# Two thirds of the recurrence's output projection taken out of the merge and done between the steps of the prompt's attention

## The chip, the cores and the metric

The kernel runs on one core of one Trainium2 chip. The metric is the device time of one execution in microseconds, the median of several. The engines are TensorE (PE, with its weight loads shown apart as PEld), VectorE (DVE), ScalarE (ACT), GpSimd (POOL) and SyncE (SP), which issues most of the transfers.

## What is computed

One step of a decoder layer with two branches over the same rows: latent attention (MLA) and a recurrence (RWKV-7). There are 1040 prompt rows (16 meta tokens and 1024 of the prompt) and 8 rows of a decoding batch. Both branches are projected to the model's 1024 columns, gated and added. Cut to what matters here:

```python
o_mla = attend(...).reshape(B, T, 8 * 64) @ lw['w_o_mla']          # 512 -> 1024
o_rwkv, wkv_new = rwkv_branch(rw_cols, shift0, wkv0, lw)           # a scan over the tokens
o_rwkv = o_rwkv.astype(x.dtype) @ lw['w_o_rwkv']                   # 512 -> 1024
g_mla, g_rwkv = jnp.split(jax.nn.sigmoid(gate_in), 2, axis=-1)
x = x + (g_mla * o_mla + g_rwkv * o_rwkv) @ lw['w_out']
x = x + jnp.square(jax.nn.relu(rms_norm(x, g_ffn) @ lw['w_up'])) @ lw['w_down']
```

The change concerns the product of the recurrence's rows with `w_o_rwkv`. The meta tokens' rows are dropped before the merge, so 1032 rows enter it; they lie along the free axis (the "columns" below), in three blocks `NBQ` of 344.

## The kernel before

Products keep float32's precision by splitting each operand into a rounded high part and a remainder: the cast to the high part is ScalarE's (`wh<-raw`, L119, or L1035), the remainder is a subtraction, mostly POOL's (L110), and `mm3` issues three products, high by high, low by high, high by low. All products that go through the helper have the line L102, so they are told apart by the tile they write.

The part of the program around the change has two stages. **The mixed stage.** `rwkv` (L808) walks through the segments of the recurrence (`for s in range(LAST + 1)`, segments 0 to 8; all but the last have two chunks of 64 tokens) and `chain_step` (L650) through the chunks. A chunk is a chain: the `zu` products read the state, VectorE and ScalarE copy and add, and the state of the next chunk comes out of the last `zu` group. `solve`, `solve2` and `prep` get later segments ready (`sv`, `sc` products) with VectorE's help. `post` (L690) normalizes a finished segment's rows and writes them to `orw` in DRAM; post(s-1) is called in segment s.

Beside it `fill` (L1982) advances the prompt's attention `mla` (L1365), one step for each step of `rwkv`. Attention goes head by head (8 heads) and block by block (3 blocks of up to 384 queries). `mla_head` loads and splits a head's K and Q, through one staging buffer (`mst`, tile `qkst`). `mla_max` (L1088) finds the row maxima of the *next* head: its `mx` products go into a PSUM pool of two banks, VectorE reduces them, and a transposed copy `mt` puts the maxima into Q's extra row. `mla_block` (L1133) computes the scores `at` in another pool of two banks, ScalarE takes the exponential to `P`, and the `pv` product sums over V in a single bank. When the recurrence is done, `fill` is emptied. A tile scheduler puts each engine's instructions in order when the kernel is built, by data dependencies, free buffers and the priorities set with `hi(...)`: the recurrence's (1500 to 3500) above the attention's. On the chip each engine then executes its own queue in that fixed order and waits at its head where something is not ready.

**The merge** (`stage_merge`, L1394). `rows(i, b, ...)` loads block i of the attention's rows `om` (b = 0, divided by the softmax sums through a broadcast load `rl`) or of the recurrence's rows `orw` (b = 1), and splits them into `x`. `chunk(m, i0, i1)` does output block m of 8 for the row blocks i0 to i1: it loads and splits two weights (`w_o`, the attention's and the recurrence's half), loads the gates `gt` and takes their tanh on ScalarE (L1443), makes 12 products of 344 columns per branch and row block, multiplies each result with its gate on VectorE, adds the two on POOL and splits the sum for the next product. The first three m run blocks 0 and 1 first (`MB` = 3, `MC` = 2), then block 2; the other five run all three blocks.

## Time and profile before

| | us |
|---|---|
| three runs | 2014.69, 2030.19, 2030.24 (median 2030.19) |
| the profiled execution, its own time | 2013.76 |
| its span in the trace | 2011.8 (41,500 instructions) |
| TensorE busy | 1854.2 |
| VectorE / POOL / ScalarE busy | 1319.1 / 953.3 / 737.0 |
| mean granted TensorE clock | 0.957 of full |

The span is the profiled execution from its first to its last instruction; times of instructions are counted from its start. TensorE's products are pipelined, so a busy share of 92% does not mean that it runs at its peak, and the busy times by tile of one stretch can add up to more than the engine's own. A granted clock of 1.00 is 2.4 GHz, 0.50 is 1.2 GHz.

### The profile page before, as it was taken

The page shows a single profiled execution, that of the slowest core. Times are in us where ns is not written, and L with a number is a line of the kernel's source. Part 1 is how long each engine was busy: PE and PEld are TensorE (multiplying, and loading weights), DVE is VectorE, ACT ScalarE, POOL GpSimd, SP SyncE. Part 2 cuts the span into 40 slices and gives each one's busy share as a digit, 9 for nine tenths or more (in the row PEclk, how much of TensorE's full clock was granted, in tenths as well). Part 3 has the DMA queues.
Part 4 walks back from the last instruction along what each step waited for, and adds up shares of the span by engine and source line. Part 5 has one row for each costly group of instructions (what it writes and reads, how often), then busy time and mean ns, then how long its engine had stood idle before and what let it go on. Part 6 is the DMA issues. An engine that isn't in the chain of part 4 may idle for free.

```text
span 2011.8 us, 41500 instructions
## 1 busy us (share of the span) xinstructions
PE 1854.2 (92%) x16508; PEld 1710.7 (85%) x16508; DVE 1319.1 (66%) x2212; ACT 737.0 (37%) x1516; POOL 953.3 (47%) x791
## 2 busy tenths in 40 slices
PE   8999889999989978989898899999999988999996
PEld 6989778889989866767666799999999988999995
DVE  6743556665446577877854554586666667869896
ACT  5442211122212234444445533533333333443354
POOL 4353534443313243334542543465565574645766
PEclk9998999999989978999899999999999998999998
DMA  4355555653433353332324733534443468454422
GB/s 167 115 189 179 181 208 185 216 195 135 142 102 113 92 141 79 82 92 47 84 62 121 233 116 128 167 106 149 143 147 131 147 185 301 138 170 133 130 85 85
DMA packets 209921, 282.64 MB, mean 140 GB/s; under 512 B 52960, under 2 KB 124536, under 8 KB 209600
## 3 DMA queue, kind: packets, MB, share of 16 engines
q1 hardware_dynamic: 198784, 237.66, 38.0%
q0 software_dynamic: 10944, 42.33, 6.3%
q8 instruction: 130, 2.13, 0.4%
q14 instruction: 63, 0.52, 0.1%
HBM read 197.61 MB, written 82.31 MB: 139 GB/s over the span
## 4 chain that ended last, share of the span: by engine, by line
PE 45%; DVE 13%; DMA 6%; issue 5%; POOL 4%; ACT 2%; SPq 1%; DVEq 0%; POOLq 0%; ACTq 0%
PE u L102 23%; PE mm L102 13%; DVE pr L576 2%; PE sv L102 2%; PE pv L102 2%; PE at L102 1%; PE zu L102 1%; DVE T L578 1%; POOL ul L110 1%; DVE x L1744 1%; PE sc L102 1%; PE mx L102 1%; DVE mpart L1117 1%; DVE c L1684 1%; ACT uh L1035 1%
## 5 line engine op out<-in xcount | busy, mean ns | idle before, releaser
L102 PE MATMUL mm<-h,wh 128*128 128x344 f32 (+1 forms) x1680 | 423.2, 334 | 17.2 <-ACT wh L119 8.3
L102 PEld LDWEIGHTS mm<-h,wh 128*128 128x128 f32 x1680 | 299.4, 194 | 29.2 <-ACT wh L119 8.4
L102 PE MATMUL mm<-h,wl 128*128 128x344 f32 (+1 forms) x840 | 275.7, 331 | 0.0
L110 POOL TENSOR_TENSOR wl<-raw,wh 128x512 fp32r<-128x512 f32 (+2 forms) x71 | 92.6, 1305 | 176.3 <-ACT wh L119 172.1
L102 PEld LDWEIGHTS mm<-h,wl 128*128 128x128 f32 x840 | 162.5, 194 | 2.5 <-issue 1.6
L119 ACT CAST wh<-raw 128x512 fp32r<-128x512 f32 (+2 forms) x118 | 70.6, 606 | 230.8 <-PE mm L102 165.0
L102 PE MATMUL u<-B11h,uh 128*128 128x258 f32 x448 | 130.3, 291 | 9.9 <-DVE c L1695 4.9
L102 PE MATMUL u<-T1h,uh 128*128 128x258 f32 x416 | 119.0, 286 | 11.7 <-ACT acc L1790 9.9
L102 PE MATMUL u<-B11h,ul 128*128 128x258 f32 x448 | 128.4, 286 | 0.0
L102 PE MATMUL u<-B11l,uh 128*128 128x258 f32 x448 | 128.1, 286 | 0.0
L102 PE MATMUL u<-T1l,uh 128*128 128x258 f32 x416 | 118.5, 285 | 0.0
L102 PE MATMUL u<-T1h,ul 128*128 128x258 f32 x416 | 118.3, 284 | 0.0
L1685 ACT ACTIVATE c<-c 128x516 f32<-128x516 f32 x64 | 40.7, 636 | 204.5 <-DVE c L1684 204.5
L102 PE MATMUL u<-B21h,uh 128*128 128x258 f32 x384 | 108.9, 284 | 1.5 <-ACT r L1670 1.0
L102 PE MATMUL u<-B21h,ul 128*128 128x258 f32 x384 | 108.7, 283 | 0.0
L102 PE MATMUL u<-B21l,uh 128*128 128x258 f32 x384 | 108.4, 282 | 0.0
L1267 DVE STREAM_TRANSPOSE T<-R 128x2560 f32<-128x2560 f32 (+1 forms) x32 | 80.9, 2558 | 34.6 <-DMA R<-cache,ix 32.6
L102 PE MATMUL mm<-x,wh 128*128 128x344 f32 x384 | 91.9, 325 | 9.4 <-ACT wh L119 5.5
L102 PEld LDWEIGHTS u<-B11h,uh 128*128 128x128 f32 x448 | 86.5, 193 | 12.7 <-ACT uh L1035 6.2
L102 PE MATMUL pv<-P,V 128*65 128x272 f32 (+5 forms) x288 | 93.0, 416 | 1.8 <-ACT P L1152 1.7
L1229 POOL DMA_INDIRECT R<-cache,ix x64 | 62.6, 978 | 63.0 <-PE dc L102 47.3
L102 PE MATMUL mm<-m,wh 128*128 128x344 f32 x384 | 90.3, 323 | 2.0 <-ACT wh L119 2.0
(511 smaller groups left out, 5761.8 us busy)
## 6 DMA issues: line engine op xcount, KB each, us to landing
raw<-w_in SPq DMA_DIRECT2D x70, 256.0 KB
A<-w_up SPq DMA_DIRECT2D x70, 256.0 KB
adT<-ts SPq DMA_DIRECT2D x64, 258.0 KB
br<-adT SPq DMA_DIRECT2D x64, 258.0 KB
a<-w_down SPq DMA_DIRECT2D x64, 256.0 KB
adB<-c SPq DMA_DIRECT2D x48, 258.0 KB
br<-adB SPq DMA_DIRECT2D x48, 258.0 KB
z<-zs SPq DMA_DIRECT2D x8, 1280.0 KB
```

Source lines behind the costliest of these rows:

```text
L102: self.nc.tensor.matmul(out, l, r, start=start, stop=stop)
L110: (eng or self.nc.vector).tensor_tensor(lo, src, hi.bitcast(F32), ALU.subtract)
L119: nc.scalar.copy(hi, raw)
L576: nc.vector.tensor_tensor(q, T[q_, :, 0:i + 1], Nt[q_, 0:i + 1, i].rearrange("p (o j) -> p o j", o=1).to_broadcast([q_.stop - q_.start, 8, ...
L578: nc.vector.tensor_reduce(T[q_, :, i], q, AX.X, ALU.add)
L1035: self.nc.scalar.copy(hi, src)
L1117: nc.vector.tensor_reduce(t[:m, j:j + 1], ps[:m, :n], AX.X, ALU.max)
L1229: self.nc.gpsimd.indirect_dma_start(out=R[:, 4 * i:4 * i + 4].rearrange("p a c -> p (a c)"), out_offset=None, in_=self.I["cache"].rearrang ...
L1267: nc.vector.transpose(t.rearrange("p j x k -> p x j k"), R[:, :, c0:c1].rearrange("p x (j c) -> p x j c", c=32))
L1684: V.scalar_tensor_tensor(c, c, 0.0, self.r2[:, ns], ALU.max, ALU.mult)
L1685: A.activation(c, c, AF.Square)
L1744: V.tensor_tensor(v2(t), ps, v2(t), op)
```

## The change

A new generator `rwkv_out` computes `w_o`'s recurrence half times the recurrence's rows for row blocks 0 and 1 (of three), output block by output block: it loads the rows from `orw` and splits them (`owh`, `owl`), loads and splits a weight for each of the 8 output blocks, makes 12 products of 344 columns into a tile `ow`, has ScalarE copy the result to `oo`, and writes that to a new DRAM buffer `ows`. `fill` advances it at every fourth step of the attention. A block may begin only when the rows it needs are written: `post` sets `ow_ready` to 1 behind segment 3's call and to 2 behind segment 6's.

In the merge, `chunk` no longer loads the recurrence's half of the weight unless the last row block is among its blocks, makes the recurrence's 12 products for row block 2 alone, and for blocks 0 and 1 loads the finished product from `ows` (`oa`) and multiplies it with the gate in one pass of 688 columns. That is 192 products of 576 fewer in the merge, and 192 more in the mixed stage.

The PSUM pools of the mixed stage change with it: instead of two banks for `at`, two for `mx` and one for `pv` there are four for `at`, `mx` and `ow` together and one for `pv`.

```diff
@@ -60,6 +60,8 @@
 RP = 300
 MC = 2
 G0, G1, F1, S0, MST = 8, 1000, 1, 5, 1
+
+OWS = (3, 6)
 RPS = (("sc", 1), ("sv", 1), ("zu", 1))
 
 V_GMIX, V_GQ, V_GKV, V_MU, V_W0, V_A0, V_KK, V_KA, V_RK, V_LNW, V_LNB, V_GFFN, V_GFIN = (
@@ -177,6 +179,7 @@
         self.om = d.tile([128, 4, TPAD], F32, name="om")
         self.qr = d.tile([2, 128, TPAD], F32, name="qr")
         self.dsm = d.tile([544, NS], F32, name="dsm")
+        self.ows = d.tile([KD, 128, 2 * 344], F32, name="ows")
         self.xs = d.tile([128, KD, TQ], F32, name="xs")
         self.ads = {n: d.tile([2 * KD, 128, HT], F32, name="ad" + n) for n in XO[0]}
 
@@ -838,6 +841,7 @@
         get = lambda s: prep[s] if s <= LAST else (None, none)
 
         def post(s):
+            self.ow_ready = (s > OWS[0]) + (s > OWS[1])
             if s >= 0:
                 with hi(1500):
                     self.post(prep[s][0])
@@ -1104,7 +1108,7 @@
             t = self.asm.tile([128, 3], F32, tag="mp", name="mpart") if len(bl) > 1 else None
             dst = mx[:m, i - i0, 0:1]
             for j, (k0, n) in enumerate(bl):
-                ps = self.ps_mx.tile([128, 512], F32, tag="mx", name="mx")
+                ps = self.ps_at.tile([128, 512], F32, tag="at", name="mx")
                 last = j == len(bl) - 1
                 self.mm(ps[:m, :n], Q[0:96, 128 * (i - i0):128 * (i - i0) + m], Kk[0][0:96, k0:k0 + n], True, not last)
                 if last:
@@ -1390,6 +1394,29 @@
                 pass
             V = nxt
 
+    def rwkv_out(self, ctx):
+
+        nc = self.nc
+        p = self.pool(ctx, "owp")
+        for i in range(2):
+            while self.ow_ready <= i:
+                yield
+            n0, n = NBQ[i]
+            hi, lo = (p.tile([128, 4, n], F32R, tag="x" + t, name="ow" + t) for t in "hl")
+            for k in range(4):
+                raw = self.rp.tile([128, 512], F32, tag="raw", name="raw")[:, :n]
+                nc.sync.dma_start(raw, self.orw[:, k, META + n0:META + n0 + n])
+                self.split(hi[:, k], lo[:, k], raw, nc.gpsimd)
+            for m in range(KD):
+                w = self.load_k(self.I["w_o"][m][:, 4:], 4, eng=nc.gpsimd)
+                ps = self.ps_at.tile([128, 512], F32, tag="at", name="ow")[:, :n]
+                for k in range(4):
+                    self.mm3(ps, w[k][0], w[k][1], hi[:, k], lo[:, k], k == 0, k == 3)
+                o = p.tile([128, 344], F32, tag="o", name="oo", bufs=2)
+                nc.scalar.copy(o, ps)
+                nc.sync.dma_start(self.ows[m, :, n0:n0 + n], o)
+                yield
+
 
     def stage_merge(self, ctx):
 
@@ -1429,22 +1456,27 @@
             for i in range(3):
                 with self.tc.high_priority(RP):
                     a = rows(i, 0, 0, 3)
-                    r = rows(i, 1, 0, 4)
+                    r = rows(i, 1, 0, 4) if i == 2 else None
                     z = rows(i, 0, 3, 4)
                 x.append(([a[j] + z[j] for j in range(2)], r))
 
             def chunk(m, i0, i1):
-                w = [self.load_k(I["w_o"][m][:, 4 * b:4 * b + 4], 4) for b in range(2)]
+                w = [self.load_k(I["w_o"][m][:, 4 * b:4 * b + 4], 4) for b in range(1 + (i1 == 3))]
                 a, z = NBQ[i0][0], sum(NBQ[i1 - 1])
                 gt = [gp.tile([128, TQ], F32, tag=f"gt{b}", name="gt")[:, :z - a] for b in range(2)]
                 for b in range(2):
 
                     nc.sync.dma_start(gt[b], self.gts[2 * m + b][:, a:z])
                     nc.scalar.activation(gt[b], gt[b], AF.Tanh, scale=0.5)
+                w_ = min(z, 688) - a
+                if w_ > 0:
+                    oa = gp.tile([128, 688], F32, tag="oa", name="oa")[:, :w_]
+                    nc.sync.dma_start(oa, self.ows[m, :, a:a + w_])
+                    nc.vector.scalar_tensor_tensor(gt[1][:, :w_], gt[1][:, :w_], 1.0, oa, ALU.add, ALU.mult)
                 for i in range(i0, i1):
                     n0, n = NBQ[i]
                     t = [gt[b][:, n0 - a:n0 - a + n] for b in range(2)]
-                    for b in range(2):
+                    for b in range(1 + (i == 2)):
                         self.proj(w[b], x[i][b], 4, lambda _, n0, n, ps: nc.vector.scalar_tensor_tensor(
                             t[b], t[b], 1.0, ps, ALU.add, ALU.mult), [(0, n)])
                     nc.gpsimd.tensor_tensor(t[0], t[0], t[1], ALU.add)
@@ -1982,14 +2014,19 @@
                 def fill():
                     yield from gates
                     ca.close()
-                    psum(cm, ("at", 2), ("mx", 2), ("pv", 1))
+                    psum(cm, ("at", 4), ("pv", 1))
                     with tc.high_priority(HP):
                         k.mla_open(cm)
                     smp = k.sample_step(c)
+                    ow = k.rwkv_out(cm)
                     for i, _ in enumerate(k.mla()):
                         if k.rwkv_done:
                             next(smp, None)
+                        if i % 4 == 3:
+                            next(ow, None)
                         yield
+                    for _ in ow:
+                        pass
                     for _ in smp:
                         yield
                 fill = fill()
```

**What moves in the queues.** The scheduler places the moved products, and with them everything else, anew. The first engine is TensorE. The counts give how many instructions of the attention (the masks' products included) and of `ow` stand in its queue ahead of the first `zu` product of a chunk:

| ahead of | before: at, mx, pv | after: at, mx, pv, ow |
|---|---|---|
| segment 4, first chunk | 96, 62, 25 | 75, 54, 21, 0 |
| segment 5, second chunk | 193, 96, 53 | 75, 54, 21, 0 |
| segment 7, second chunk | 344, 148, 96 | 185, 96, 53, 96 |
| segment 8, its only chunk | 489, 192, 138 | 185, 96, 53, 96 |
| the merge | 504, 192, 144 | 504, 192, 144, 192 |

In the rows below a name's number tells one tile from the next, `idb` is the identity, `mb` a mask, and `UV`, `BKt`, `AR`, `Sm`, `BK`, `TT` are the recurrence's operands; the helper's line L102 is L104 in the changed file.

The first place is in the recurrence's segment 5, on TensorE. Before, attention products stand between the chunk's `zu` and `sv`:

```order
L102 MATMUL at_10890<-Qh02_7627,Kh0_7623 128x272
L102 MATMUL at_10890<-Ql0_7631,Kh0_7623 128x272
L102 MATMUL at_10890<-Qh02_7627,Kl0_7633 128x272
L102 LDWEIGHTS idb_120
L102 MATMUL at_10890<-mb_7639,idb_120 128x128
L102 MATMUL zu_9128<-UV_8233,BKt_8232 64x64 x8
L102 MATMUL sv_9061<-AR_8844,BK_8851 128x128 x4
L102 MATMUL pv_10742<-P_10830,V_9458 65x272
L102 MATMUL at_10905<-Qh02_7627,Kh0_7623 128x256
L102 MATMUL at_10905<-Ql0_7631,Kh0_7623 128x256
L102 MATMUL at_10905<-Qh02_7627,Kl0_7633 128x256
```

After, the queue holds only the recurrence there, from segment 4's first chunk on (`zu_9625` opens the second chunk of segment 5), up to the first `ow` products, and the next `at` stands behind those:

```order
L104 MATMUL sv_9062<-AR_8845,BK_8852 128x128 x4
L104 MATMUL zu_9129<-UV_8234,BKt_8233 64x64 x8
L104 MATMUL sv_9068<-AR_8845,BK_8852 128x128 x4
L551 MATMUL sc_9332<-cst_120,BK_8852 128x128 x4
L104 MATMUL zu_9129<-Sm_8012,UV_8234 64x64 x8
L104 MATMUL sv_9074<-AR_8845,BK_8852 128x128 x4
L104 MATMUL zu_9625<-UV_8234,Sm_8012 64x64 x8
L104 MATMUL ow_9609<-owh_9585,wh_9604 128x344
L104 MATMUL ow_9609<-owl_9586,wh_9604 128x344
L104 MATMUL at_9682<-Qh11_7627,Kh1_7622 128x384
```

The attention's instructions of three chunks have moved behind the first `ow`.

The second place is where the attention goes from one head to the next, on TensorE, late in the stage. Before (seven more `at` tiles of this head stand ahead of these rows; `mx_11726` is the first product that needs the following head's K and Q):

```order
L102 MATMUL pv_11758<-P_11791,V_11467 65x384
L102 MATMUL at_11811<-Qh01_7626,Kh0_7623 128x256
L102 MATMUL at_11811<-Ql0_7631,Kh0_7623 128x256
L102 MATMUL at_11811<-Qh01_7626,Kl0_7633 128x256
L102 LDWEIGHTS idb_120
L102 MATMUL at_11811<-mb_7639,idb_120 128x128
L102 MATMUL mx_11726<-Kh1_7624,Qh10_7628 128x256
L102 LDWEIGHTS idb_120
L102 MATMUL mx_11726<-mb_7639,idb_120 128x256
L102 MATMUL mx_11738<-Kh1_7624,Qh10_7628 128x256
```

After, at a change of head in the stretch behind the recurrence (`mx_12115` is the first product with the next K and Q):

```order
L104 MATMUL pv_11988<-P_12049,V_11205 65x272
L104 MATMUL at_12107<-Qh00_7623,Kh0_7621 128x384
L104 MATMUL at_12107<-Ql0_7629,Kh0_7621 128x384
L104 MATMUL at_12107<-Qh00_7623,Kl0_7631 128x384
L104 LDWEIGHTS idb_121
L104 MATMUL at_12107<-mb_7637,idb_121 128x128
L104 MATMUL pv_11988<-P_12062,V_11205 65x272
L104 MATMUL pv_11988<-P_12077,V_11205 65x144
L104 MATMUL pv_11988<-P_12085,V_11205 65x16
L104 MATMUL pv_12106<-P_12112,V_11856 65x384
L104 MATMUL mx_12115<-Kh1_7622,Qh10_7626 128x256
```

Here one `at` tile of the new head stands ahead of the first `mx`, where eight did before, and the two kinds alternate from there.

The third place is the start of the merge, on ScalarE. Before (`ov` is the attention's last copy, `x1000` and `x1100` casts of the merge's rows, L710 to L715 the last segment's normalization):

```order
L1156 COPY ov_12096<-pv_12029 65x272
L1035 CAST x1000_12199<-raw_12189 128x1032
L1035 CAST x1100_12205<-raw_12203 128x1376
L710 ACTIVATE sq_10923<-y_10717 128x512
L1443 ACT_TABLE_LOAD
L1443 ACTIVATE gt_12269<-gt_12269 128x688
L1443 ACTIVATE gt_12270<-gt_12270 128x688
L1443 ACTIVATE gt_12349<-gt_12349 128x688
L1443 ACTIVATE gt_12350<-gt_12350 128x688
L714 ACT_TABLE_LOAD
L714 ACTIVATE sq_10923<-sv_10933,eps_62 128x512
```

After:

```order
L1160 COPY ov_12485<-pv_12418 65x272
L1470 ACT_TABLE_LOAD
L1470 ACTIVATE gt_12640<-gt_12640 128x688
L1470 ACTIVATE gt_12641<-gt_12641 128x688
L1470 ACTIVATE gt_12689<-gt_12689 128x688
L1470 ACTIVATE gt_12690<-gt_12690 128x688
L1039 CAST x0000_12554<-raw_12544 128x1032
L1039 CAST x0003_12568<-raw_12558 128x344
L1484 ACTIVATE m00_12520<-gt_12640 128x344
```

Two casts and the normalization with its table loads have left this place; a table load and four `gt` now stand ahead of the first cast `x0000`. SP's queue grows from 944 to 988 rows, 40 of its new transfers ahead of the merge: 8 loads of `orw`, 16 of `w_o` and 16 stores to `ows`.

## Rows read from the trace of the kernel before

**Rows 1.** Page, part 1: busy time of each engine, share of the span, instructions.

```profile
PE 1854.2 (92%) x16508; PEld 1710.7 (85%) x16508; DVE 1319.1 (66%) x2212; ACT 737.0 (37%) x1516; POOL 953.3 (47%) x791
```

**Rows 2.** By stretch: start:end length, busy PE PEld DVE ACT POOL, clock, DMA share, GB/s.

```profile
790.60:837.50 46.90, 45.28 (x598) 35.24 (x597) 38.38 (x102) 24.25 (x65) 19.32 (x18) 1.00 0.37 91
837.50:892.00 54.50, 47.36 (x591) 36.67 (x590) 39.37 (x103) 26.18 (x68) 21.31 (x20) 0.94 0.38 97
892.00:945.20 53.20, 48.17 (x584) 36.85 (x583) 43.00 (x118) 24.63 (x69) 20.29 (x19) 0.98 0.21 45
...
1015.00:1070.40 55.40, 51.46 (x506) 38.82 (x504) 33.77 (x89) 25.16 (x72) 19.84 (x22) 0.94 0.22 62
```

**Rows 3.** Timeline of TensorE, first groups of chunks: start, length, in brackets idle before.

```profile
837.52 0.73 PE L102 MATMUL zu<-UV,Sm 128*64 128x64 f32 x4
...
911.51 0.69 PE L102 MATMUL zu<-UV,Sm 128*64 128x64 f32 x16
...
1015.06 0.34 PE L102 MATMUL zu<-UV,Sm 128*64 128x64 f32 x4
...
1088.92 0.28 PE L102 MATMUL zu<-UV,Sm 128*64 128x64 f32 x2
...
1096.98 0.69 PE L102 MATMUL zu<-Sm,UV 128*64 128x64 f32 x16 [1.31 <-DVE PT L684]
1097.81 0.42 PE L102 MATMUL mm<-x,wh 128*128 128x344 f32 x1
```

**Rows 4.** TensorE alone in that stretch, by tile: at, mx, pv, zu, sv in order.

```profile
1015.00:1070.40 55.40, 27.06 (x118) 0.94 0.22 62
1015.00:1070.40 55.40, 12.21 (x46) 0.94 0.22 62
1015.00:1070.40 55.40, 21.10 (x66) 0.94 0.22 62
1015.00:1070.40 55.40, 3.86 (x80) 0.94 0.22 62
1015.00:1070.40 55.40, 6.68 (x192) 0.94 0.22 62
```

**Rows 5.** VectorE over 790.6 to 945.2, tile mx, then tile mt.

```profile
sum 154.60, DVE 34.69; mean DVE 11.56
sum 154.60, DVE 9.90; mean DVE 3.30
```

**Rows 6.** A stretch at low clock (columns as Rows 2), and a zu group in it.

```profile
738.00:779.00 41.00, 32.10 (x364) 25.42 (x364) 25.03 (x70) 10.57 (x28) 15.27 (x16) 0.62 0.29 71
...
741.08 1.12 PE L102 MATMUL zu<-Sm,UV 128*64 128x64 f32 x16
```

**Rows 7.** Timeline of ScalarE and POOL: a head's K and first block of Q.

```profile
1038.00 1.07 ACT L1035 CAST Kh<-qkst 96x1048 fp32r<-96x1048 f32 x1 [0.63 <-PE at L102]
1039.49 2.43 POOL L110 TENSOR_TENSOR Kl<-qkst,Kh 96x1048 fp32r<-96x1048 f32 x1
...
1046.29 0.51 ACT L1035 CAST Qh<-qkst 96x384 fp32r<-96x384 f32 x1 [0.42 <-DMA qkst<-qr]
```

**Rows 8.** The merge: mm products by stretch, longest wait, timeline, chain.

```profile
1097.80:1204.00 106.20, 94.77 (x576) 0.97 0.56 175
1150.00:1200.00 50.00, 50.00 (x319) 1.00 0.46 152
...
PE mm L102 <- ACT wh L119: 5.5, 1, 5.5
...
1103.85 1.28 ACT L1443 ACT_TABLE_LOAD   x1
...
1110.79 0.78 ACT L1443 ACTIVATE gt<-gt 128x688 f32<-128x688 f32 x1 [1.32 <-DMA gt<-gts]
...
1116.86 5.29 DMA rl<-rls
...
1122.30 2.07 POOL raw L1423
```

## The prediction

> **What bounds the kernel now.** Begin with the page's head: TensorE is busy for 92% of the span [rows 1], so work that only changes its place gains nothing unless it lands where TensorE waits. Next take the busy time of each engine by stretch. In the three segments of the recurrence between 790.6 and 945.2 us TensorE is busy for 45 to 48 us of 47 to 55 us, and VectorE, the second engine, for 38 to 43 us [rows 2]. Two independent streams fill that time: the recurrence, a dependent chain of small products (`zu`, `sv`, `sc`) with much VectorE work between them, and the prompt's attention (`at`, `mx`, `pv`), which fills the chain's gaps. The stage ends only when both are done, and in the trace they end together: the last chunk's last product starts at 1096.98, the merge's first at 1097.81 [rows 3]. The merge then keeps TensorE full (50.00 us of 50.00), 576 products in 106.2 us [rows 8]. So the merge is bound by TensorE, and the stage before it by TensorE as long as attention and recurrence run side by side. The order of each queue is fixed when the kernel is built, so what runs beside what is read from the order, and how long it takes from the trace.
>
> **The change, part by part.** I follow TensorE's queue from the first place where it departs.
>
> *The start of the hold.* The recurrence's chunk that opens segment 4 starts at 837.5 [rows 3]. Ahead of it the new order has 21 `at`, 8 `mx` and 4 `pv` fewer (the table of counts). At the prices derived under the tail these are 3.8 + 1.7 + 2.0 = 7.5 us of TensorE. Between no gain, where the chain sets the pace, and all of it, I take half: the chunk starts at 834 (830 to 838).
>
> *The hold.* From there to the second chunk of segment 5 the new order has no attention at all. The next `at` stands behind the first `ow` products, and these need the recurrence's rows of segments 0 to 3 to be written to DRAM, read back and split. So for three chunk steps TensorE has the recurrence alone. In the trace these steps took 911.5 - 837.5 = 74.0 us with the attention beside them [rows 3]. Alone they cannot be faster than VectorE: it was busy for 38.38 + 39.37 + 43.00 = 120.8 us over three segments [rows 2], at most 34.7 + 9.9 = 44.6 us of that for the attention's maxima [rows 5], which leaves 76.2 us, 25.4 us a segment and 38 us for one and a half. VectorE reached 120.8/154.6 = 78% in those stretches, because the chain makes it wait; 38/0.78 is 49, and I take 50 us. Bounds: 38 to 74.
>
> Here a page speaks against the change. The trace first: between 738 and 779 us, where TensorE was busy for only 32.1 of 41 us, the mean granted clock was 0.62, most of it the lower level, 1.2 GHz; a group of 16 `zu` products took 1.12 us there and 0.69 us at full clock [rows 3, 6]. The Trainium skill, TensorE: Matmul & The Clock Gate, in its part 1 on the clock gate, says that the throttled clock is the default and that activity releases it. The hold would then run at 1.2 GHz throughout. Five groups a chunk cost 5 x 0.43 = 2.2 us more, 6.5 us over three steps, and the forecast would rise by that. I leave it out, because the 78% already comes from a chain with such waits.
>
> *The shared stretch.* From the second chunk of segment 5 to the second of segment 7 both orders run both streams. Before: 1015.1 - 911.5 = 103.6 us [rows 3] with 151 `at`, 52 `mx`, 43 `pv`. Now 110, 42 and 32, and 96 `ow`. By the prices below that is 7.3 + 2.1 + 5.5 = 14.9 us of attention less and 15.1 us of `ow` more: 104 us. Bounds 89 (`ow` hidden in the chain's waits) to 119 (the lost attention gives nothing back).
>
> *The end of the recurrence.* At the second chunk of segment 7 the second hold begins, since the second half of `ow` needs the rows up to segment 6. Three chunks are left until the first `ow` of that half. The last chunk of the trace took from 1088.9 to the end of its last group, 1096.98 + 0.69 = 1097.7 us: 8.8 us [rows 3]; three of those are 26, with posts and the last solve between them I take 27 us. Bounds 23 to 45. The recurrence then ends at 834 + 50 + 104 + 27 = 1015 us, 82 us earlier than before, and at that point 319 of 504 `at`, 96 of 192 `mx`, 91 of 144 `pv` and 96 `ow` are still to do.
>
> *The tail.* The nearest rows are those of 1015 to 1070.4, where the attention was nearly alone. TensorE's busy time by tile is 27.06 + 12.21 + 21.10 + 3.86 + 6.68 = 70.9 us (products overlap) in 55.4 us [rows 4], so each of those us stands for 0.78 us. That is 0.179 us for one of 118 `at`, 0.207 for one of 46 `mx`, and 0.50 for a `pv`, which is two instructions in the trace (66 there). The tail: 57.1 + 19.9 + 45.5 = 122.5 us, and `ow` at the merge's own price of 50/319 = 0.157 us [rows 8] adds 15.1, in all 137.6 us. Two corrections. That stretch had a mean clock of 0.94 [rows 2]; full clock takes off about 3 us in 55, 7 in all. But `at` and `mx` now draw on one pool of four banks and stand alternately in the queue. At the change of a head only one `at` tile stands ahead of the next head's first `mx`, where before several stood there (the order's second place). That `mx` needs the next K and Q. In the trace, from the cast of K to the end of the first cast of Q took 1038.0 to 1046.8, 8.8 us, with the split of K and a load in between [rows 7]. One `at` tile and the four last `pv` cover about 3 us, so some 5 us stay open at each of three heads; at the fourth, `ow` products cover it. I take 14 us: 137.6 - 7 + 14 = 145 us. Bounds: 120 (full clock, no boundary waits) and 172 (four full waits). The stage ends at 1160 us, where it ended at 1097.8: **62 us later**.
>
> *The merge.* It loses 192 of its 576 products, 30.1 us [rows 8]. It also loses the wait of 5.5 us for a weight's cast [rows 8]: ScalarE had to do the last segment's rows and their table loads there, and these are now long done. Against this, ScalarE's new order has one table load and four `gt` behind the attention's last copy, 1.28 + 4 x 0.8 = 4.5 us [rows 8], then the first cast of `x`. Before, the first two blocks of `x` were cast ahead of that copy. The copies and splits of `raw` follow one another for three blocks, with 2.1 us for a POOL product and 5.3 us for a slow `rl` load as the trace's sizes [rows 8]. TensorE waits some 9 us. The merge also moves more bytes in less time: per output block, two weights of 256 KB, two `gt` of 528 KB and one `oa` of 352 KB in about 48 x 0.157 = 7.5 us is 256 GB/s, against 175 over the merge before [rows 8]; I take 3 us for late loads. The removed product passes on VectorE pay for the new pass over `oa`. Together: 106.2 - 30.1 - 5.5 + 9 + 3 is 82.6; less 3 us for the half-clock part that the merge had (mean clock 0.97 over 106.2 us [rows 8]), 79 us: **27 us shorter**. Bounds 22 to 34.
>
> *What costs nothing.* ScalarE (16 copies, 21 casts) and POOL (24 splits) do the rest in a stage where they are busy for less than 27 of 47 to 55 us [rows 2]. Their cover is that slack; gone, it would cost their 20 to 30 us. SP's queue gets 40 more transfers before the merge; the `raw` loads wait on it for the rows' landing, and segment 7's `Ns` stores queue behind them. That is inside the 78%.
>
> **Sum.** +62 - 27 = +35 us. The profiled execution took 2013.8 us by its own time, which gives 2049. The runs shown took 2014.7, 2030.2 and 2030.2; with the profiled one, two of four are 16 us above the others, which one profile cannot explain. I add half, 8 us: **2057 us**.
>
> **Rivals.**
> *No difference.* The recurrence alone may run at VectorE's floor (38 us), the shared stretch may hide `ow` (89 us), and the tail may run at 122 us. Then the stage ends at 834 + 38 + 89 + 27 + 122 = 1110, 12 us later, and the merge takes back 27: -15 us, about 2007 with the offset. For it speaks that the attention stretch was TensorE-bound at 51 of 55 us; against it that all three must come at their ends. With one or two of them the result lies between -15 and +20.
> *Faster.* One mechanism: the hold frees the chain entirely, and its three steps take the 8.8 us of the last chunk each, 26 us. With the shared stretch at 89 and the tail at 128, the stage ends at 834 + 26 + 89 + 27 + 128 = 1104 and the net is +6 - 27 = -21 us, 2001. It decides from a stage end before 1105. Against it: VectorE's 38 us do not fit in.
> *Slower still.* Every change of a head waits the full 8.8 us (tail 172) and the merge's loads, whose stage reached 0.56 of the DMA engines at 175 GB/s [rows 8], become its bound with no gain left beyond 22 us. +62 + 27 - 22 = +67, about 2089.
>
> **How the numbers follow.** My forecast, +20 to +55, gets 0.55, slower still 0.14, no difference 0.24, faster 0.07. About 1%, 20 us, is what a measurement of this kernel tells from no change. So slower 0.69, same 0.24, faster 0.07. The range leaves one in ten out at each side: from the middle of the no-difference case, 2014, to just above the slower one, 2096; these take in 16 us between like runs.
>
> **What would show it.** The hold: no `at` product for some 50 us from about 835 us, and the clock falling there. The recurrence's last `zu` near 1015 us, and 60% of the `at` products after it. The tail: some 145 us with TensorE waiting at heads 4 to 7 for the cast of Q. The merge's first product near 1170 and its length near 79 us. The forecast is wrong if the recurrence ends before 990 us, or if the tail takes under 125 us.

## The result, and the profile after

The changed kernel takes 2138.86 us (median of 4 runs, 2132.66 to 2139.32) against 2024.21 us before (4 runs, 2014.69 to 2030.24): the ratio is 1.058, 95% interval 1.054 to 1.062. The profiled execution took 2139.21 us with a span of 2137.1. It was forecast slower, at 2057, with a range to 2096: the direction was right, the size was not. The loss is 115 to 125 us, not 35.

One label of the table of counts has to be put right first, and with it the sentence that all segments but the last have two chunks: the segment with a single chunk is the first, and the row "segment 8, its only chunk" is segment 8's second chunk. The places and counts stand.

The page's first row, which answers [rows 1]:

```profile
PE 1904.3 (89%) x16508; PEld 1753.9 (82%) x16508; DVE 1320.4 (62%) x2201; ACT 753.0 (35%) x1549; POOL 972.8 (46%) x813
```

TensorE has the same 16508 instructions and is busy for 50 us more, since part of them now runs at a lower clock, and idle for 75 us more (232.8 against 157.6 us of the span). The stretches, with the columns of [rows 2]: the first hold, the shared stretch, the second hold, the merge, and the tail in a second answer:

```profile
837.60:909.00 71.40, 50.83 (x622) 43.87 (x623) 41.85 (x95) 20.68 (x49) 26.71 (x27) 0.55 0.35 88
909.00:1013.00 104.00, 92.18 (x1116) 75.48 (x1116) 78.02 (x191) 42.70 (x111) 52.05 (x52) 0.93 0.31 83
1013.00:1068.60 55.60, 34.26 (x490) 29.30 (x485) 20.82 (x48) 15.50 (x39) 19.80 (x25) 0.56 0.21 54
...
1220.20:1327.00 106.80, 71.91 (x386) 66.81 (x387) 53.07 (x78) 45.12 (x71) 47.98 (x38) 0.82 0.64 188
...
1068.00:1220.20 152.20, 132.12 (x746) 100.27 (x743) 50.11 (x128) 68.47 (x178) 36.40 (x29) 0.90 0.28 80
```

Both holds are where the order put them, and in both the clock is near its lower level: 0.55 and 0.56, where [rows 2] showed 0.94 to 1.00. But they are long. TensorE's timeline, which answers [rows 3], has their edges:

```profile
837.58 1.26 PE L104 MATMUL zu<-UV,Sm 128*64 128x64 f32 x12 [4.25 <-DVE Sm L649]
...
907.41 1.12 PE L104 MATMUL zu<-UV,Sm 128*64 128x64 f32 x16
908.46 0.66 PE L104 MATMUL ow<-owh,wh 128*128 128x344 f32 x1
...
1020.07 1.12 PE L104 MATMUL zu<-UV,Sm 128*64 128x64 f32 x16
...
1034.68 0.27 PE L805 MATMUL sc<-cst,yb 8*128 8x8 f32 x1 [4.86 <-DMA yb<-sy]
...
1068.14 0.65 PE L104 MATMUL ow<-owh,wh 128*128 128x344 f32 x1
...
1235.56 0.65 PE L104 MATMUL mm<-x,wh 128*128 128x344 f32 x1 [15.38 <-ACT x L1039]
```

The attention's last product ends at 1220.2, and TensorE then waits 15.4 us for the merge's first operand. The steps of the sum against the trace, each from the times above (and 1326.9, the end of the merge's last product; before, 1097.9 and 1204.3):

| step | forecast, us | measured, us | off by |
|---|---|---|---|
| start of the first hold | 834 | 837.6 | +4 |
| first hold | 50 | 907.4 - 837.6 = 69.8 | +20 |
| shared stretch | 104 | 1020.1 - 907.4 = 112.7 | +9 |
| end of the recurrence, to the next `ow` | 27 | 1068.1 - 1020.1 = 48.0 | +21 |
| tail | 145 | 1220.2 - 1068.1 = 152.1 | +7 |
| mixed stage against before | +62 | +122.3 | +60 |
| merge against before | -27 | 106.7 - 106.4 = +0.3 | +27 |
| the rest of the kernel | 0 | 810.2 - 807.5 = +2.7 | +3 |

So three terms carry the miss: the two holds, 41 us, and the merge, 27 us. The 4 us of the first row arose ahead of the stage, where the input projection ended at 726.4 instead of 722.3; counted from there the hold began 4 us sooner than before, as forecast.

### The profile page after: what moved, and what is told of

The parts are those of the page before. It is cut to its first block, busy times and chain, and to the rows that moved or that the text cites. A ratio compares the mean times of both kernels' runs of the same rounds, so it can differ in the third digit from the quotient of the medians.

```text
span 2137.1 us, 41651 instructions
## 1 busy us (share of the span) xinstructions
PE 1904.3 (89%) x16508; PEld 1753.9 (82%) x16508; DVE 1320.4 (62%) x2201; ACT 753.0 (35%) x1549; POOL 972.8 (46%) x813
## 5 line engine op out<-in xcount | busy, mean ns | idle before, releaser
L104 PE MATMUL mm<-h,wh 128*128 128x344 f32 (+1 forms) x1680 | 424.3, 334 | 18.8 <-ACT wh L121 7.7
L104 PEld LDWEIGHTS mm<-h,wh 128*128 128x128 f32 x1680 | 300.0, 195 | 31.2 <-ACT wh L121 7.8
L104 PE MATMUL mm<-h,wl 128*128 128x344 f32 (+1 forms) x840 | 275.8, 331 | 0.0
L112 POOL TENSOR_TENSOR wl<-raw,wh 128x512 fp32r<-128x512 f32 (+2 forms) x85 | 109.2, 1287 | 212.4 <-ACT wh L121 203.8
L104 PEld LDWEIGHTS mm<-h,wl 128*128 128x128 f32 x840 | 162.6, 194 | 2.5 <-issue 1.6
L121 ACT CAST wh<-raw 128x512 fp32r<-128x512 f32 (+2 forms) x131 | 78.9, 607 | 242.4 <-PE mm L104 162.6
L104 PE MATMUL u<-B11h,uh 128*128 128x258 f32 x448 | 129.2, 289 | 8.0 <-DVE c L1727 3.6
L104 PE MATMUL u<-T1h,uh 128*128 128x258 f32 x416 | 119.2, 287 | 13.0 <-ACT acc L1822 11.2
L104 PE MATMUL u<-B11h,ul 128*128 128x258 f32 x448 | 128.0, 286 | 0.0
L104 PE MATMUL u<-B11l,uh 128*128 128x258 f32 x448 | 127.7, 285 | 0.0
L104 PE MATMUL u<-T1l,uh 128*128 128x258 f32 x416 | 118.6, 285 | 0.0
L104 PE MATMUL u<-T1h,ul 128*128 128x258 f32 x416 | 118.5, 285 | 0.0
L104 PE MATMUL u<-B21h,uh 128*128 128x258 f32 x384 | 108.9, 284 | 1.6 <-ACT r L1702 1.2
L104 PE MATMUL u<-B21h,ul 128*128 128x258 f32 x384 | 108.8, 283 | 0.0
L104 PE MATMUL u<-B21l,uh 128*128 128x258 f32 x384 | 108.4, 282 | 0.0
L104 PE MATMUL mm<-x,wh 128*128 128x344 f32 x256 | 68.1, 350 | 34.0 <-ACT x L1039 27.1
L104 PEld LDWEIGHTS u<-B11h,uh 128*128 128x128 f32 x448 | 85.9, 192 | 10.1 <-ACT uh L1039 4.5
L104 PE MATMUL mm<-m,wh 128*128 128x344 f32 x384 | 91.0, 325 | 3.5 <-ACT wh L121 3.5
L104 PE MATMUL pv<-P,V 128*65 128x272 f32 (+5 forms) x288 | 90.6, 408 | 2.3 <-ACT ov L1160 2.2
```

The source lines that it names most:

```text
L104: self.nc.tensor.matmul(out, l, r, start=start, stop=stop)
L112: (eng or self.nc.vector).tensor_tensor(lo, src, hi.bitcast(F32), ALU.subtract)
L121: nc.scalar.copy(hi, raw)
```

## The experiments

In what follows "stage" is the time from the input projection's last product to the last product of recurrence, attention and `ow`, and "merge" the time from there to the merge's last product, both from the runs' profiled executions. Medians, with the kernel before run beside them (`oldpools` was run twice, the last four rows once each). The diffs show changed lines alone; what lies between them is left out.

| kernel | median, us | before beside it | ratio, 95% interval | stage, us | merge, us |
|---|---|---|---|---|---|
| before | | | | 375.6 | 106.4 |
| changed | 2138.86 | 2024.21 | 1.054 to 1.062 | 493.8 | 106.7 |
| oldmerge | 2144.21 | 2022.72 | 1.057 to 1.065 | 500.0 | 110.5 |
| newmerge | 2029.23 | 2022.72 | 1.000 to 1.005 | 384.6 | 104.0 |
| newmerge_pl | 2015.71 | 2019.73 | 0.995 to 1.000 | 388.4 | 83.9 |
| after_pl | 2130.10 | 2019.73 | 1.048 to 1.059 | 501.9 | 87.9 |
| oldpools | 2106.87 | 2020.93 | 1.039 to 1.046 | 461.5 | 108.2 |
| tail | 2081.75 | 2022.72 | 1.027 to 1.035 | 432.2 | 109.9 |
| tail22 | 2070.25 | 2022.72 | 1.019 to 1.028 | 423.9 | 112.0 |
| late22_pl | 2079.64 | 2020.93 | 1.027 to 1.032 | 446.8 | 87.8 |
| noatt | 1972.38 | 2020.93 | | 339.7 | 101.7 |
| noatt_fill | 1977.57 | 2018.61 | | 349.2 | 98.9 |
| nofill | 2145.88 | 2019.73 | | 504.6 | 107.2 |
| filler | 2148.73 | 2019.73 | | 502.7 | 105.8 |

**What sets the pace of the holds.** The kernel before, with the attention taken out:

```diff
-                    for i, _ in enumerate(k.mla()):
-                        if k.rwkv_done:
-                            next(smp, None)
-                        yield
+                    k.no_att(cm)          # om and ls filled with ones
+                    while not k.rwkv_done:
+                        yield
```

> The kernel before without the prompt's attention (its outputs are filled with constants): the recurrence has TensorE and VectorE to itself for its whole length. Theory V, the chain with its solves sets its own pace and the attention only filled its waits: the three chunks from segment 4's first to segment 5's second take 60 to 75 us, as with the attention beside them (74.0) and as in the changed kernel's hold (69.8), and the last chunks of segments 7 and 8 take some 45 us as in its second hold. Theory W, the step of the prediction, that the chain alone keeps VectorE at 78%: 50 us or less for the three chunks.

The same three chunks by the profile of `noatt`, and the rest up to the recurrence's end at 1062.7:

```profile
824.00:894.80 70.80, 50.70 (x606) 43.91 (x606) 38.56 (x88) 23.47 (x48) 21.68 (x21) 0.52 0.33 83
...
989.30:1062.70 73.40, 47.00 (x497) 41.82 (x497) 28.67 (x59) 27.16 (x46) 27.63 (x24) 0.60 0.38 93
```

Alone the three chunks take 70.8 us, beside the attention 74.0 [rows 3], in the hold 69.8. Theory V holds for them; W falls. Two of the kernels below, `tail` and `late22_pl`, have no hold at this place, and there the same chunks run beside the attention:

```profile
831.60:901.00 69.40, 64.48 (x784) 49.93 (x783) 54.05 (x140) 35.30 (x93) 32.75 (x30) 0.95 0.42 107
838.20:905.30 67.10, 61.17 (x765) 46.59 (x764) 52.00 (x134) 31.47 (x85) 27.19 (x27) 0.97 0.39 96
```

The last three chunks took 73.4 us alone, 82.6 beside the attention (1015.06 to 1097.7 [rows 3]), and 57.2 in the changed kernel's second hold (to the recurrence's end at 1077.3). V's 45 us for this end was too little. In `noatt` the merge's first products already stand in that stretch, with 17.96 us of TensorE from 1033.7 on, so 73.4 is not the chain's time alone.

Without the attention the stage is 339.7 us against 375.6, and the whole kernel is 49 us faster. So all of the attention, some 202 us by the prediction's prices (504 x 0.179 + 192 x 0.207 + 144 x 0.50), costs on balance 36 us of the stage and 49 us of the whole; the higher clock that comes with it is part of this balance. TensorE was busy, but the recurrence's chain set the pace and the attention lay mostly in its waits. In the first hold the chain gains 4 us from having the engines to itself, while 97 `at`, 34 `mx` and 28 `pv`, 38 us by the same prices, are put off and come later at full price. In the second it gains 25 us of 82.6.

**Whether the clock sets it.** Idle products in the holds, which keep the clock up. `nofill` has a free bank but no products, `filler` has 4 behind each of three steps:

```diff
+                if (s, c) in FILL:        # (4,0) (4,1) (5,0) (7,1) (8,0)
+                    for z, n in zip((t[0], u.UV[:, :, 0, 0:64], t[1]), NF):    # (4, 4, 4); nofill: (0, 0, 0)
+                        fl = self.ps_fl.tile([128, 512], F32, tag="fl", name="fl")
+                        for j in range(n):
+                            self.mm(fl[:64, :256], z[:, 0, :], z, True, True)
```

> The control of the run filler: the changed kernel with three banks for at, mx and the moved products and one free bank. The holds are in the order as before (no attention between segment 4's second chunk and the first moved product in segment 5's second). Both theories: that stretch as in the changed kernel, some 52 us, at a clock of 0.50 to 0.55.

> As nofill, with 12 idle float32 products of 256 columns put behind each of five chunks in the holds (segment 4's two, segment 5's first, segment 7's second, segment 8's first), 4 behind each of three steps of the chain, writing a bank that nothing reads. In the hold of segments 4 and 5 TensorE does the same work and 36 products more. Theory K, the hold is paced by TensorE at half clock: the products release the clock (0.8 or more) and the stretch from segment 4's second chunk to the first moved product falls from some 52 us to 36 to 45. Theory V, it is paced by VectorE and the chain's latencies: 50 us or more, since the products can only delay it.

`noatt_fill` does the same in the recurrence alone, with 3 behind each step of every chunk from segment 3 on:

> The run noatt with idle products that nothing reads: 3 float32 products of 256 columns behind each of three steps of every chunk from segment 3 on, 9 a chunk, so that TensorE is busier and its clock higher while the recurrence's own work and order stay. In noatt the seven chunks from segment 4's first to segment 7's second took 165 us (824.0 to 989.3) at a clock of 0.50 to 0.64. Theory K, the half clock paces the chain: at a clock of 0.8 or more the same chunks take 145 us or less. Theory V, VectorE's steps and the chain's handovers pace it: 158 us or more, whatever the clock.

By stretch, first `nofill` and `filler` (segment 4's two chunks and segment 5's first), then `noatt_fill` (the same three, then the chunk after them and the next three):

```profile
829.80:850.80 21.00, 19.21 (x166) 15.54 (x166) 13.25 (x30) 7.32 (x19) 7.92 (x8) 0.58 0.66 163
850.80:875.70 24.90, 15.97 (x309) 14.07 (x308) 18.10 (x51) 7.25 (x16) 7.59 (x7) 0.64 0.05 7
875.70:894.50 18.80, 13.20 (x136) 11.41 (x136) 8.79 (x18) 6.61 (x16) 9.14 (x10) 0.50 0.70 185
```

```profile
838.80:859.20 20.40, 19.77 (x183) 14.42 (x184) 12.73 (x30) 7.11 (x19) 7.99 (x8) 0.75 0.67 168
859.20:884.60 25.40, 21.79 (x341) 15.57 (x340) 18.81 (x52) 7.69 (x18) 7.53 (x7) 0.87 0.06 7
884.60:904.00 19.40, 15.76 (x165) 12.42 (x164) 9.03 (x18) 6.17 (x15) 9.13 (x9) 0.82 0.67 174
```

```profile
817.50:875.70 58.20, 47.22 (x654) 35.31 (x654) 37.47 (x89) 23.79 (x48) 21.74 (x21) 0.86 0.40 101
875.70:899.80 24.10, 19.24 (x311) 14.20 (x310) 17.94 (x52) 14.40 (x22) 8.03 (x8) 0.85 0.06 8
899.80:971.50 71.70, 53.76 (x738) 39.43 (x738) 42.31 (x96) 15.00 (x33) 27.33 (x31) 0.67 0.24 59
```

The products raise the clock from about 0.58 to 0.82, and in `filler` the three chunks take 65.2 us against 64.7 in `nofill`: no gain, as theory V says. (The stretch that the expectations name, from segment 4's second chunk to the first moved product, takes 54.4 us in `filler` and 49.7 in `nofill`.) In `noatt_fill` they take 58.2 us against 70.8 at 0.52, a gain of 12.6, and the seven chunks 154.0 against 165.3, between the two theories' bounds. The idle products stand in the chain's way themselves (16 us of them in the 58.2, 19 in the 65.2), and in `noatt_fill` groups of the solves' `sv` and `sc` products stand elsewhere in TensorE's queue than in `noatt`, though its expectation had the order unchanged. So neither number is the clock's price alone: no gain and 12.6 us are what the two pairs show, and the price itself stays open. `nofill` and the changed kernel differ by 5 us in the same stretch at nearly the same clock, with one bank less and another order. In neither run do the three chunks come to the 50 us of the forecast.

**Without the holds.** In `tail` the moved products are made only when the attention's steps have all been emitted, `tail22` has the old pools besides:

```diff
-                        if i % 4 == 3:
-                            next(ow, None)
```

> The changed kernel, but the moved products are made only when the attention's steps have all been emitted, so nothing of the attention stands behind products that wait for the recurrence's rows; pools and merge are as in the changed kernel. In the build's order the two stretches without attention are gone (183 at ahead of segment 5's second chunk, 319 ahead of segment 7's second). Theory 1, the two holds are what lengthens the mixed stage: the stage ends at about 1098 + 15 (the moved products) + 5 to 15, and with a merge of 100 to 106 us the time is 2030 to 2060 us, 80 to 110 below the changed kernel's 2139. Theory 2, the moved products and the shared pool cost this wherever the products stand: 2100 us or more.

> As the run tail, but with the PSUM pools of before: two banks for at and the moved products, two for mx. Theory 1 (the holds): within 15 us of the run tail. The term of 14 us that the prediction gave to the shared pool at changes of head expects this one 10 to 15 us faster than tail; if the pool costs nothing, they agree within 8 us.

`tail` comes out between its two theories, at 2081.75. The holds are gone and 62 us of the stage with them; that bears out theory 1 for the stage, but its numbers were missed, because `ow` at the end takes far more than its 15 us. `tail22`, at 2070.25, is 11.5 us faster than `tail`, as the term for the shared pool had it; TensorE's waits for the next head's Q, 13.0 us in `tail`, are 0.6 in `tail22`. In `tail22`, TensorE by stretch: `ow`, the wait for the merge, the merge:

```profile
1086.90:1145.80 58.90, 42.47 (x308) 0.86 0.60 181
1145.80:1165.40 19.60, 0.29 (x3) 0.58 0.47 128
1165.40:1258.10 92.70, 73.09 (x386) 0.83 0.58 180
```

The stretch of the 192 products takes 58.9 us where the merge's price makes 30. They keep TensorE busy for 36.87 us of it, it waits 12.6 us for the cast of a weight, and the recurrence's last products lie in the same stretch. So work that was put at the stage's end still pays for its own loads and casts. Then the merge's rows are not ready for another 19.6 us; the load `rl` that they need comes late here too, at 1156.06, which the part on the merge takes up.

**The shared pool.** The changed kernel with the old pools alone:

```diff
-                    psum(cm, ("at", 4), ("pv", 1))
+                    psum(cm, ("at", 2), ("mx", 2), ("pv", 1))
-                ps = self.ps_at.tile([128, 512], F32, tag="at", name="mx")
+                ps = self.ps_mx.tile([128, 512], F32, tag="mx", name="mx")
```

> The changed kernel with the PSUM pools of before alone (two banks for at and the moved products, two for mx). Both holds are still in the order. If the shared pool costs its 10 to 14 us at changes of head: 2122 to 2132. If the holds are due to the shared pool, 2090 or less. If neither, 2139.

32 us faster than the changed kernel: more than the 10 to 14 that were forecast for the changes of head, and the holds stay (no `at` from 812.3 to 922.2), so they are not due to sharing with `mx`; the moved products sit in the ring of banks of `at` either way. The `mx` products, which have their own ring here, go on until 851.0, 39 us after the last `at`. That fits a ring held by the products that wait; moved products with a bank to themselves were not tried. TensorE's waits in the tail, changed kernel and then `oldpools` (total, times, longest), and its stretch:

```profile
PE mx L104 <- ACT Qh L1039: 17.7, 4, 5.6
```

```profile
PE mx L104 <- ACT Qh L1039: 0.4, 1, 0.4
```

```profile
1059.00:1184.80 125.80, 124.06 (x751) 94.59 (x747) 51.85 (x128) 67.91 (x178) 36.62 (x29) 0.97 0.35 96
```

The tail has the same products and takes 125.8 us instead of 152.2. Of those 26 us, 17 are the waits for the next head's Q; the clock, 0.97 instead of 0.90, is the likely rest.

**The merge.** Each half of the change alone: `oldmerge` keeps the new mixed stage and gives the merge all its products back; `newmerge` keeps the mixed stage of before, with no moved products at all (`ows` is filled with a constant), and takes the new merge.

```diff
 oldmerge:
-                    r = rows(i, 1, 0, 4) if i == 2 else None
+                    r = rows(i, 1, 0, 4)
-                w_ = min(z, 688) - a
+                w_ = 0
-                    for b in range(1 + (i == 2)):
+                    for b in range(2):
 newmerge, in place of the products:
+        z = p.tile([128, 688], F32, tag="o", name="oo")
+        nc.gpsimd.memset(z, 0.5)
+        for m in range(KD):
+            nc.sync.dma_start(self.ows[m], z)
```

> The mixed stage of the changed kernel, moved products included, but the merge of before, which makes all 576 products again and does not read the moved ones' results. Theory A, the merge's gain was lost because the 192 products had covered the preparation of the attention's rows: the time stays within 10 us of the changed kernel's 2139 (2129 to 2149). Theory B, the merge is bound by its products and it is slow for another reason (half clock, late loads): 30 us longer, 2160 to 2175.

> The mixed stage and the pools of before with no moved products (the buffer that the merge reads is filled with a constant, so two thirds of the recurrence's projection are left out), and the merge of the changed kernel. The mixed stage ends as before, with part of the rows prepared ahead of its end. Theory A (cover): the merge is 10 to 20 us shorter than before, because its first row blocks are prepared ahead here, but not by the full 30: 2000 to 2015 against 2024. Theory B (the merge is bound by its products): 25 to 30 us shorter, 1990 to 2000. A third result, no shorter at all, would say that the loads of oa and gt bind the merge.

192 products more cost `oldmerge` 5 us, inside theory A's band, and 192 fewer gain `newmerge` nothing: the third result of its expectation. Whether the loads of `oa` and `gt` bind it, as that result had it, is for the next two runs. SyncE's queue in `newmerge` shows what was late. The attention ends at 1110.9 there. The sums of the first row block are stored at 1072.48, but their broadcast load `rl` stands in the queue behind the attention's end and behind `gt` and `oa`:

```profile
1072.48 0.77 SPq L1431 DMA_DIRECT2D rls<-lt  x1
...
1110.88 0.40 SPq L1455 DMA_DIRECT2D gt<-gts  x1
1111.34 0.41 SPq L1460 DMA_DIRECT2D oa<-ows  x1
...
1115.16 1.30 SPq L1434 DMA_DIRECT2D rl<-rls  x2
...
1126.60 0.65 PE L104 MATMUL mm<-x,wh 128*128 128x344 f32 x1 [15.72 <-ACT x L1039]
```

It is the same in the changed kernel, where the attention ends at 1220.2. In the kernel before, and in `oldmerge`, which keeps that kernel's merge, the load follows its store. The rows are those of the changed kernel, of before and of `oldmerge`:

```profile
1164.38 0.75 SPq L1445 DMA_DIRECT2D rls<-lt  x1
...
1224.36 1.32 SPq L1448 DMA_DIRECT2D rl<-rls  x2
```

```profile
1066.70 0.77 SPq L1418 DMA_DIRECT2D rls<-lt  x1
...
1069.85 1.28 SPq L1421 DMA_DIRECT2D rl<-rls  x2
```

```profile
1157.28 0.78 SPq L1445 DMA_DIRECT2D rls<-lt  x1
1159.28 1.26 SPq L1448 DMA_DIRECT2D rl<-rls  x2
```

What differs is memory: `op0` and `op1` each lost 11008 bytes a partition with the recurrence's rows, `gp` gained 5504 for `oa`, and the pools behind slid to other addresses. That these lie over buffers which the attention holds to its last product is inferred; the traces show no addresses. `newmerge_pl` and `after_pl` put them back:

```diff
-            gp, op2, op1, rl_, rw, op0 = pl("gp", 2), pl("op2"), pl("op1"), pl("rl"), pl("rw", 2), pl("op0")
+            gp, op2, op1, oap, rl_, rw, op0 = pl("gp", 2), pl("op2"), pl("op1"), pl("oap", 4), pl("rl"), pl("rw", 2), pl("op0")
-                    oa = gp.tile([128, 688], F32, tag="oa", name="oa")[:, :w_]
+                    oa = oap.tile([128, 688], F32, tag="oa", name="oa")[:, :w_]
```

> The run newmerge with one change of memory: the pool of oa (four buffers, 11008 bytes a partition) stands between op1 and rl, where op1 lost as many bytes with the recurrence's rows, so that rl, raw and op0 lie at the addresses of before. Theory P, placement: the merge gained nothing in newmerge because its rows' buffers had slid onto buffers that the attention holds to its end, so that the rl loads (1115 us, behind the attention's end at 1111) came late; here the first rl loads come ahead of the attention's end again, TensorE's wait of 15.7 us at the merge's start is gone, the merge takes 78 to 86 us from the attention's end, and the time is 2000 to 2012 us (newmerge 2029). Theory C, the removed products were the only cover: no change, 2022 or more.

> The changed kernel with the same change of memory as newmerge_pl. The build's order has the loads of rl for row block 0 three attention blocks ahead of the end and those of block 1 around it. Theory P: 15 to 25 us faster than the changed kernel, 2114 to 2124. Theory C: within 6 us of 2139.

The same places in `newmerge_pl`, where the attention ends at 1117.8:

```profile
1074.77 0.77 SPq L1431 DMA_DIRECT2D rls<-lt  x1
1076.72 2.15 SPq L1434 DMA_DIRECT2D rl<-rls  x2
...
1109.95 1.15 SPq L1434 DMA_DIRECT2D rl<-rls  x2
...
1117.73 0.94 PE L104 MATMUL mm<-x,wh 128*128 128x344 f32 x2
```

`rl` follows its store by 2 us, the merge starts with the attention's end, and it takes 83.9 us instead of 104.0; in `after_pl` 87.9 instead of 106.7. The loads of `oa` and `gt` are still there, so they are not what bound it. Placement is the cause of the merge's lost gain in both mixed stages. In these two runs `oa` also has four buffers instead of two, but `oldmerge`, without any `oa` and with the pools of before, starts its merge without a wait too. So theory A's account of `oldmerge`, that the removed products had been the cover, met its band for another reason. In total `after_pl` is 9 us faster than the changed kernel, less than the 15 to 25 expected, because its stage is 8 us longer; and `newmerge_pl`, with two thirds of the recurrence's projection left out, is 4 us below the kernel before, not 8 to 20, because its stage is 13 us longer than before, as that of `newmerge` is 9. The recurrence takes as long as before there (within 2 us), and the attention ends 12 and 10 us behind it; why was not tried.

**All three causes at once.**

```diff
-OWS = (3, 6)
+OWS = (6, 7)
 and the edits of oldpools and after_pl
```

> The changed kernel with three parts undone or moved: the moved products wait for segment 6's and segment 7's post instead of segment 3's and 6's (so that their rows are long written when the attention reaches them), the PSUM pools are those of before, and the merge's pools lie as in after_pl. In the build's order the first hold is gone (185 at ahead of segment 5's second chunk), the second is left for segment 8's two chunks. Theory 1 (holds, pool and placement are the causes): 2035 to 2065. Theory 2 (the moved products cost this wherever they stand): 2090 or more.

2079.64: above the band, 27 us better than `oldpools`. The merge gains its 20 us (108.2 to 87.8), and the stage 15 us, since the first hold is nearly gone but the second is left (no `at` from 1025.6 to 1071.4). No version that makes all products beats the kernel before. `newmerge_pl` wins 4 us with the moved products left out altogether; its merge is 22 us shorter, and the longer stage takes most of that back.

## Why the prediction was right in its sign and wrong in its size

**The hold** was the first step that failed, and its fault is in one division. The prediction took VectorE's own work for the recurrence, 76 us in three segments or 38 in the hold, and `noatt` bears that out: 38.56 us. But it divided it by VectorE's share of 78% in stretches where the attention's maxima were part of that share. Without them VectorE was busy for 41.85 of 71.4 us in the hold, 59%, and for 38.56 of 70.8 in `noatt`, 54%. The time that the chain spends elsewhere did not shrink with the other stream gone. The upper bound of the term, 74 us (the chain gains nothing), was nearly the truth, and `noatt` shows that this is the chain's own pace at the clock that it gets alone. How much of that pace is the clock stays open.

**The end of the recurrence** was priced too low as well: 8.8 us a chunk came from the trace's very last chunk, which has no solve, no `prep` and no later post beside it and ran at a clock of 1.00. The three chunks also carried posts and the decoding rows' step (the wait of 4.86 us for `yb` is one), ran at 0.50, and took 48 us to the next `ow`. Its upper bound of 45 was too low. How the 21 us divide among these was not tried. The recurrence ended at 1077.3 instead of 1015, and neither of the prediction's two signs of being wrong came, since both looked for a shorter stage.

**The merge** failed for a reason that was nowhere in the working. The prediction saw that the merge's casts came later in ScalarE's queue, took it for an exchange of places worth 9 us, and let the rest of the 30 us stand. It did not ask why rows that used to be prepared ahead no longer were. The place to ask is SyncE's queue, where `rl` stands behind the attention's end. With the addresses put back the merge is 22.5 us (`newmerge_pl`) and 18.5 us (`after_pl`) shorter than before, about the term's lower bound of 22.

**What held.** Both holds, the falling clock in them and 63% of the `at` products behind the second. The start of the first hold. The tail's prices: 145 forecast, 152.1 measured, and the changes of head, forecast at 14 us, measured at 17.7 with waits of up to 5.6 us for the cast of Q, against "some 5 us at each". The shared stretch: 112.7 us, within its bounds, with TensorE busy for 92.18 of 104.00 us in the window shown. With every step at its measured size the sum closes: 35 + 4 + 20 + 9 + 21 + 7 + 27 + 3 = 126, against 2139.2 - 2013.8 = 125.4.

**The rivals.** No rival had the cause. "Slower still" had the right side and a wrong mechanism: the changes of head waited for 17.7 us, not 35, and the merge was not bound by its loads. "No difference" and "faster" both needed a chain that is freed by the hold, and `noatt` shows that it is not.

**The clock.** The hold's granted clock of 0.55 agrees with the rule of the Trainium skill, TensorE: Matmul & The Clock Gate, part 1, that the throttled state is the default and activity lifts it; idle products lifted it to 0.82. The 6.5 us that the prediction derived and left out counted the `zu` groups alone, and these did take 17.81 us of TensorE in the hold against 11.79 in the same chunks before. But in the hold all of the recurrence's products run at that clock. With idle products the same stretch gained nothing in one kernel and 12.6 us in the other, so the clock may be a good part of the term's error of 20 us or little of it; the runs do not decide.

## What to carry to other kernels

When two streams share the engines, run one of them alone before pricing its separation: here the attention, 202 us of TensorE, cost the stage 36 us, so what was held back of it in the first hold was lost nearly in full, though TensorE's 92% looked like the bound. Products that wait for slow data and stand in the queue ahead of another stream hold that stream up (no `at` for 80 us here), so place them where their data is long there; the ring of banks that they shared with it is the likely reason that the scheduler kept the two in that order. And after an edit that changes the size of a pool, look at the next stage's first loads in the queue: here a few KB of shift decided whether 20 us of preparation ran ahead.

## What was not expected of the hardware

The recurrence's chain ran as fast at a clock of 0.52 to 0.55 (70.8 and 69.8 us for three chunks) as at 0.95 with the attention between its products (74.0). A lower granted clock is thus no sign by itself of how much time is lost: with idle products between, the same stretch was no shorter at 0.82 in one kernel (65.2 against 64.7) and 12.6 us shorter at 0.86 in the other.
